# Left operands at fixed products, rows' functions one product later, and a scan that loads behind attention's stores

## The chip, the cores and the metric

The kernel runs on one core of a Trainium2 chip. The metric is the device time of one execution in microseconds (us); less is better. TensorE (PE) multiplies matrices into PSUM; VectorE (DVE), ScalarE (ACT) and GpSimd (POOL) work on rows; SyncE (SP) issues most of the DMA transfers, and POOL a few.

## The reference

One inference step of a hybrid layer, over a prompt of 1024 tokens and a running stream of 64 tokens with a cache, 1088 tokens in all. The width is 1024.

```python
xn = _rmsnorm(x, p['norm_mix_w'])
proj = xn @ p['w_in']
z, xbc, dt_raw, q, k, v, gate_ssm, gate_att = jnp.split(proj, ...)
xbc_c, conv_new = _causal_dwconv(conv_past, xbc, ...)          # then silu, split into xs, bm, cm
y_ssm, ssm_new = _ssd_scan(xs, dt, a_neg, bm, cm, ssm_past, chunk_len)
y_ssm = _rmsnorm((y_ssm + ssm_d * xs) * jax.nn.silu(z), ssm_norm_w)   # by groups
q = _partial_rope(_rmsnorm(q, q_norm_w), q_pos); k = _partial_rope(_rmsnorm(k, k_norm_w), q_pos)
o = _rmsnorm(_diff_attention(q, k_all, v_all, q_pos, k_pos, lam), subln_w)
mix = sigmoid(gate_ssm) * (y_ssm @ w_branch_ssm) + sigmoid(gate_att) * (o @ w_branch_attn)
x = x + mix @ p['w_out']
h = _rmsnorm(x, p['norm_ffn_w']) @ p['w_up']
ha, hb = jnp.split(h, 2, axis=-1)                              # 2816 each
hc, ffn_new = _causal_dwconv(ffn_past, ha, ...)
x = x + (jax.nn.silu(hc) * hb) @ p['w_down']
```

Outputs are x of both parts, the new keys and values, the states of the scan and the last rows of both convolutions, all in float32.

## The kernel before, in words

Everything lies transposed: channels on the 128 partitions, the 1088 tokens along the row, in column halves. To keep float32 precision, an operand is split into a rounded high half and the low rest, and each product is three matmuls (high by high, high by low, low by high). A split is a cast on ACT (the high half) and a subtraction on DVE (the low half); `split` in the code.

The stages, by their time in the profile: values (up to 114 us); the pair stage (114 to 482), which makes z, q and k; attention (to 1083), beside which gates and convolutions run as filler; the scan beside filler (to 1502); branches, output projection and norm (to 1722); the way up of the feed-forward part (to 2189); the way down (to 2436); a tail of stores.

**Pairs.** The pair stage (`in_pair`), the way up (`pair`) and the way down (`down_pair`) multiply 2 × 2 blocks by a Strassen-like scheme with seven products in place of eight. A pair is two blocks of 128 output channels; each of its seven products p runs in two column halves s, so a pair has 14 half products of 12 matmuls. ACT and DVE empty the PSUM tiles into rows u1, u2 and `pre` (L622 to L634 in the pair stage, L1748 to L1770 on the way down), and PE piles a later product on a tile or reuses its bank afterwards. When a row of a pair in the pair stage is whole, `done` takes ACT's Square or Silu, DVE's running sum of squares for q and k, and a store to a scratch in HBM.

**Left operands.** The weights' blocks are loaded as w_f; three sums over them are made (ws1, ws2 and one in place), a fourth later, and seven operands are split: four into rows wh of the tag fa, the others into w_hi and w_lo. In the pair stage and on the way up `left_parts` is a generator that makes one operand after each second half product of the pair before. In the pair stage its DVE part is put off: `split_left` issues the cast at once and keeps the subtraction in `low`, and `low_left` issues it at the next operand (`lagging`). The sums are on POOL from the third pair on (L505, L506, L530, L534). On the way down `down_left` and its `lefts_at` do the same at fixed half products: load at 4, operands 0 to 3 at 8, 10, 11 and 13 of the pair before, operands 4, 5 and 6 at 0, 1 and 3 of the own.

**Rows.** `row(tag, ...)` gives a row from one of two pools: `rows_l` for the tag fa, `rows_r`, on the right side of the memory, for the others (fs for ws1 and ws2, fu for u1 and u2, fp for pre). The right side held the values' staging rows before.

**Jobs.** Between half products `take_turn` lets one or more jobs go on by a step (norm and rope of q and k, their splits); a job yields the number of turns until its next step.

**Scan.** `fetch` loads a span of inputs (tile in, three transfers), `fetch_z` the gate z, `ask` the decay rows (tile bc). `scan` begins with two spans, three asks and two gates (L1170 to L1183). The filler beside attention's end stores gate tiles g_sc (L884) and attention's output o_sc (L1103). The DMA queue of SP takes issues in program order as a scheduler lays them out, so what stands in front and waits holds the rest.

**Way down.** h is stored to the scratch h_sc during the way up. `differences_of` loads two rows of it into tiles ht (tag fb, four buffers), makes four differences on DVE (L1607 to L1610) and stores them to t_sc. The down products take right operands from h_sc (p 0, 2, 6) and t_sc (p 1, 3, 4, 5). There are three groups g of four pairs i, over 8, 8 and 6 blocks of channels; parts for a group are loaded during the last pair of the group before, as m and n tiles and, for the first part of a group, as ph (tag fb too), then split (`landed`). The couples of blocks are counted 0 to 10 in the list, and named by the index of their first block, the last three 16, 17 and 18, all of the third group.

Of the kernel before, what the change touches and what calls it, by code (L numbers as in the profile page):

```python
# [62 lines left out]
IN_ROWS = dict(fs=2, fu=2, fp=3, fc=3, fx=4, ss=2)  # L63
# [27 lines left out]
def hybrid_layer(ctx: ExitStack, tc: tile.TileContext, xT, xt, prm, cst, rope, wvd, win, wbs, wba, wout, wup, wdn,  # L91
# [386 lines left out]

    low, lagging = [], [True]

    def split_left(hi, lo, src):
        S.copy(hi, src)  # L482
        if lagging[0] and "read" in seen:
            low.append((hi, lo, src))
        else:
            V.tensor_tensor(out=lo, in0=src, in1=hi, op=ALU.subtract)  # L486

    def low_left():
        if low:
            with tc.issue_after(seen["read"].ins):  # L490
                for hi, lo, src in low:
                    V.tensor_tensor(out=lo, in0=src, in1=hi, op=ALU.subtract)
            low.clear()

    def left_parts(blocks, early=None, by=G, order=(0, 1, 2, 3)):
# [12 lines left out]
        def own(src):  # L508
            t = row("fa", "wh", R32)
            hi, lo = t[:, :n], t[:, 4 * P : 4 * P + n]  # L510
            split_left(hi, lo, src)
            return hi, lo

        def shared():
            t = [wp.tile([P, wide], R32, name=x, tag=x, bufs=2) for x in ("w_hi", "w_lo")]
            for i, src in enumerate((s1, q22)):
                hi, lo = (x[:, 512 * i : 512 * i + n] for x in t)
                split_left(hi, lo, src)
                yield 4 + i, (hi, lo)
# [16 lines left out]
        split_left(hi, lo, s2)  # L536
        yield 6, (hi, lo)

    def more_left(f):
        low_left()  # L540
        x = next(coming, None)
        if x is not None:
            left.setdefault(f, {})[x[0]] = x[1]

# [21 lines left out]
    def split_part(n, *behind):  # L566
        with ExitStack() as pins:
            for x in behind:
                pins.enter_context(tc.issue_after(x.ins))
            for s in range(2):  # L570
                hi, lo = parts[n, s]
                split(hi, lo, lo.bitcast(F32))

    def in_pair(n):
# [43 lines left out]
        for _ in range(14):  # L618
# [8 lines left out]
            else:  # L627
# [7 lines left out]
                if s == 1:  # L635
                    done(r, c)
# [63 lines left out]
    def job(fetch, scale, hi_of, hi_rows, lo_rows, keep=None):  # L700
# [4 lines left out]
        if scale is not None:  # L705
# [4 lines left out]
            yield 1  # L710
# [4 lines left out]
        yield 2 if keep is None else 3  # L715
# [120 lines left out]
    for p, s in rest:  # L836
        pairs[0].send((p, s))
        if s == 1:
            more_left(1)
            if p in LATER:  # L840
# [4 lines left out]
    for n in range(1, len(INPUT)):  # L845
        coming = in_parts(n + 1) if n + 1 < len(INPUT) else iter(())
# [9 lines left out]
        while n + 1 < len(INPUT) and len(left[n + 1]) < 7:  # L856
            more_left(n + 1)
        low_left()
        del left[n]
        if n == Q_DONE:  # L860
            beside = chain(beside, finishing("q"), finishing("k"))
    while take_turn(0):
        for _ in range(2):
            take_turn(1)
    lagging[0] = False
# [78 lines left out]
    with (tc.tile_pool(name="ak", bufs=1) as ak, tc.tile_pool(name="at", bufs=1) as at,  # L944
# [131 lines left out]
        def head_out(h, o_t, ssq, s0):  # L1076
# [15 lines left out]
            for b0 in range(0, 9, 4):  # L1092
# [9 lines left out]
                for u, t in enumerate((hi, lo)):  # L1102
                    load(out=o_sc[D * u + P * h : D * u + P * (h + 1), b0 * P : b0 * P + w], in_=t.bitcast(F32))  # L1103
# [60 lines left out]
    with (tc.tile_pool(name="sin", bufs=1) as sin, tc.tile_pool(name="sp", bufs=1) as sp,  # L1164
# [343 lines left out]

    ffn_o = tri[:, : 4 * FT].rearrange("p (f c) -> p f c", c=4)
# [144 lines left out]
    made = {}  # L1654

    def down_left(i, what):

        g, m = divmod(i, 4)
        n = P * (DOWN[g] // 2)
        if what == "load":  # L1660
            q = []
            for r in (m, m + 4):
                o = 1024 * first[g] + 2 * n * r
                w = wp.tile([P, wide], F32, name="w_f", tag="w_f", bufs=2)
                load(out=w[:, : 2 * n], in_=wdn[:, o : o + 2 * n])
                q += [w[:, :n], w[:, n : 2 * n]]
            q11, q12, q21, q22 = q
            s1, s2 = (row("fs", x)[:, :n] for x in ("ws1", "ws2"))
            G.tensor_tensor(out=s1, in0=q21, in1=q22, op=ALU.add)
            G.tensor_tensor(out=s2, in0=s1, in1=q11, op=ALU.subtract)  # L1670
            G.tensor_tensor(out=q21, in0=q11, in1=q21, op=ALU.subtract)
            made[i] = [q11, s2, q12, q21, s1, q22, q12]
            left[FT + i] = {}
            return
        src = made[i][what]
        if what < 4:
            t = row("fa", "wh", R32)
            hi, lo = t[:, :n], t[:, 4 * P : 4 * P + n]
        elif what == 6:
            hi, lo = (wp.tile([P, wide], R32, name=x, tag=x, bufs=2)[:, :n] for x in ("w_hi", "w_lo"))  # L1680
        else:
            if len(made[i]) == 7:
                made[i].append([wp.tile([P, wide], R32, name=x, tag=x, bufs=2) for x in ("w_hi", "w_lo")])
            hi, lo = (x[:, 512 * (what - 4) : 512 * (what - 4) + n] for x in made[i][7])
        if what == 3:
            G.tensor_tensor(out=made[i][6], in0=made[i][6], in1=made[i][1], op=ALU.subtract)
        with after("copy", "read"):
            split(hi, lo, src)
        left[FT + i][what] = hi, lo

    def by_token(i):
        return i % 4 in (0, 3)

    def lefts_at(i, at):

        todo = []
        if i >= 0:
# [233 lines left out]
```

## Time and profile before

| | us |
|---|---|
| median of 3 runs | 2461.15 |
| lowest and highest run | 2460.17, 2467.8 |
| the profiled execution's own time | 2447.27 |
| span of the profiled execution | 2445.5 |
| PE busy in the span | 2394.9 (98%) |
| DVE busy | 1744.6 (71%) |
| ACT busy | 1224.1 (50%) |
| POOL busy | 689.0 (28%) |

The profile shows one execution. Its rows of instructions give a start, a duration, the engine, the line and the tiles; where an engine stood idle before an instruction, the time of that and what ended it stand in brackets. A row of waits gives the instruction that waited, the one that ended it, the total us, the number and the longest. A row of transfers gives the count, the size of each and the median us from issue to landing.

### The profile page before, as it was taken

To read this page: it belongs to the slowest core of one execution; us is meant where nothing else is said; L and a number is where in the kernel's file an instruction comes from. 1 tells how busy PE (TensorE), PEld (TensorE's weight loads), DVE (VectorE), ACT (ScalarE), POOL (GpSimd) and SP (SyncE) were. 2 spreads that over 40 slices of the span, in tenths; PEclk is the share of its full clock that TensorE was granted. 3 is DMA by queue.
4 is the path that set the end of the run, shared out by engine and by line. 5 is a ranking of instruction groups with operands and counts; after the bars stand their busy time and mean duration, and the time that the engine had idled before them with its cause. 6 is when DMAs were issued, how large, how long until landed. Compare 5 with 4: busy or idle time off the path is not lost.

```text
span 2445.5 us, 49342 instructions
## 1 busy us (share of the span) xinstructions
PE 2394.9 (98%) x18744; PEld 2319.6 (95%) x18744; DVE 1744.6 (71%) x3118; ACT 1224.1 (50%) x2707; POOL 689.0 (28%) x753
## 2 busy tenths in 40 slices
PE   8999999999999999999999999999999999999998
PEld 8999989999999999998899999999999999999998
DVE  4586867668687786865787665756977777777765
ACT  7354464356565665647665554434543343352442
POOL 0023333201011010104443331013255555534444
PEclk9999999999999999999999999999999999999999
DMA  7855758665445344345897954764123423467876
GB/s 245 283 177 184 241 184 317 219 192 154 152 151 161 123 148 134 114 154 176 270 332 257 339 176 149 218 205 150 58 90 145 154 80 142 150 212 214 220 177 105
DMA packets 283088, 449.79 MB, mean 184 GB/s; under 512 B 35609, under 2 KB 189346, under 8 KB 282850
## 3 DMA queue, kind: packets, MB, share of 16 engines
q1 hardware_dynamic: 271810, 420.30, 51.8%
q0 software_dynamic: 11040, 26.34, 5.4%
q8 instruction: 147, 2.41, 0.4%
q14 instruction: 91, 0.75, 0.1%
HBM read 294.03 MB, written 152.50 MB: 183 GB/s over the span
## 4 chain that ended last, share of the span: by engine, by line
PE 66%; DMA 7%; DVE 7%; issue 3%; POOL 2%; ACT 1%; SPq 0%; POOLq 0%; DVEq 0%; ACTq 0%
PE mx L1528 9%; PE mm L162 9%; PE mm L164 9%; PE mm L163 9%; PE mm L1528 4%; PE mx L1748 4%; PE po L1071 3%; PE mx L164 2%; PE mx L162 2%; PE mx L163 2%; PE mm L1748 2%; PE mx L587 2%; PE sc L1023 2%; PE sc L1022 2%; PE pt L1051 1%
## 5 line engine op out<-in xcount | busy, mean ns | idle before, releaser
L162 PE MATMUL mm<-b,w_hi 128*128 128x272 f32 x1792 | 529.0, 295 | 0.8 <-DVE b_g L230 0.7
L164 PE MATMUL mm<-b,w_lo 128*128 128x272 f32 x1792 | 522.7, 292 | 1.8 <-DVE w_lo L156 1.8
L163 PE MATMUL mm<-b,w_hi 128*128 128x272 f32 x1792 | 520.8, 291 | 0.0
L162 PEld LDWEIGHTS mm<-b,w_hi 128*128 128x128 f32 x1792 | 337.6, 188 | 7.3 <-issue 3.8
L163 PEld LDWEIGHTS mm<-b,w_hi 128*128 128x128 f32 x1792 | 337.8, 189 | 3.3 <-issue 2.6
L164 PEld LDWEIGHTS mm<-b,w_lo 128*128 128x128 f32 x1792 | 337.1, 188 | 3.7 <-DVE w_lo L156 2.4
L912 DVE SCALAR_TENSOR_TENSOR cc<-pre,par,cc 128x272 f32<-128x272 f32 (+1 forms) x288 | 140.1, 490 | 16.4 <-ACT cc L910 13.6
L1528 PE MATMUL mx<-m,w_hi 128*128 128x272 f32 x760 | 146.1, 289 | 1.3 <-ACT m L413 1.3
L1528 PE MATMUL mx<-n,wh 128*128 128x272 f32 x1080 | 144.3, 288 | 1.9 <-DVE u L1555 1.0
L1528 PEld LDWEIGHTS mx<-n,wh 128*128 128x128 f32 x1080 | 138.5, 188 | 2.5 <-DVE u L1555 1.2
L900 POOL COPY pre<-pre 128x3 f32<-128x3 f32 x72 | 22.4, 312 | 418.3 <-DVE cc L914 186.2
L1036 ACT ACTIVATE p_t<-sc,mx 128x512 f32<-128x512 f32 (+6 forms) x144 | 106.1, 739 | 63.4 <-DVE mx L1027 30.9
L156 DVE TENSOR_TENSOR w_lo<-w_f,w_hi 128x1024 fp32r<-128x1024 f32 (+1 forms) x82 | 103.7, 1266 | 46.2 <-ACT w_hi L155 43.5
L155 ACT CAST w_hi<-w_f 128x1024 fp32r<-128x1024 f32 (+1 forms) x82 | 85.9, 1048 | 70.2 <-PE mm L163 43.0
L1528 PEld LDWEIGHTS mx<-m,w_hi 128*128 128x128 f32 x760 | 119.3, 188 | 1.5 <-ACT m L413 1.5
L1545 POOL TENSOR_TENSOR hb<-hb,cc 128x544 f32<-128x544 f32 (+2 forms) x63 | 81.8, 1312 | 101.8 <-DVE hb L1566 50.6
L482 ACT CAST w_hi<-ws 128x512 fp32r<-128x512 f32 x76 | 46.9, 617 | 126.5 <-PE mx L1528 75.0
L1528 PE MATMUL mx<-m,w_lo 128*128 128x272 f32 x380 | 109.7, 289 | 0.0
L1208 ACT ACTIVATE bc<-bc,nacum 128x128 f32<-128x128 f32 (+1 forms) x288 | 87.2, 384 | 16.1 <-POOL bc L1206 15.7
L505 POOL TENSOR_TENSOR ws<-w_f 128x512 f32<-128x512 f32 x34 | 48.5, 1425 | 154.1 <-DMA w_f<-in_win_dram 64.7
L486 DVE TENSOR_TENSOR wh<-w_f,wh 128x512 fp32r<-128x512 f32 x65 | 66.7, 1028 | 26.9 <-ACT wh L482 26.9
L1430 POOL TENSOR_TENSOR s<-s,sq 128x272 f32<-128x272 f32 x24 | 30.5, 1271 | 192.9 <-DMA out_dram<-x 131.2
(467 smaller groups left out, 7093.2 us busy)
## 6 DMA issues: line engine op xcount, KB each, us to landing
w_f<-in_win_dram SPq DMA_DIRECT2D x78, 512.0 KB, 4.2
w_f<-in_wup_dram SPq DMA_DIRECT2D x45, 512.0 KB, 3.4
bc<-a_sc SPq DMA_DIRECT2D x32, 512.0 KB, 5.9
h_sc<-hb SPq DMA_DIRECT2D x44, 272.0 KB, 2.1
ht<-h_sc SPq DMA_DIRECT2D x22, 544.0 KB, 4.8
t_sc<-ht SPq DMA_DIRECT2D x22, 544.0 KB, 2.7
out_dram<-yq POOLq DMA_DIRECT2D x44, 272.0 KB, 5.2
x_sc<-cc SPq DMA_DIRECT2D x72, 136.0 KB, 2.4
```

The lines of the kernel that those rows point to most:

```text
L155: S.copy(hi, w)
L156: V.tensor_tensor(out=lo, in0=w, in1=hi, op=ALU.subtract)
L162: PE.matmul(ps, a_hi, b_hi, start=i == 0, stop=False)
L163: PE.matmul(ps, a_hi, b_lo, start=False, stop=False)
L164: PE.matmul(ps, a_lo, b_hi, start=False, stop=i == n - 1)
L912: V.scalar_tensor_tensor(cc[:, :m], pre[:, i : i + m], cw(i), cc[:, :m], ALU.mult, ALU.add)
L1036: act(p_t[:n, :nk], sc[c][:n, :nk], AF.Exp, bias=mx[:n, c : c + 1], accum_out=dst)
L1071: PE.matmul(po[:n, :P], a_t[b // 4][:kw, b % 4 * P : b % 4 * P + n], rhs, start=b == 0, stop=b == nb - 1)
L1208: act(bc[:L, e, :L], bc[:L, e, :L], AF.Exp, bias=nacum[:L, ch, 8 * g + e : 8 * g + e + 1])
L1528: PE.matmul(ps, w[x][:, c], b[y][:, k], start=start and k == i == 0, stop=k == 3 and i == 2, skip_group_check=not start)
L1545: (V if f + 1 == FT else G).tensor_tensor(out=hb[h][:, o : o + n], in0=hb[h][:, o : o + n], in1=cc[:, d : d + n], op=ALU.mult)
L1748: PE.matmul(ps, w[y][:, c], b[z][:, k], start=start and k == j == 0, stop=k == n - 1 and j == 2, skip_group_check=not start)
```

## The change

- The tags fs and fu come from the left pool `rows_l`.
- `split_left`, `low_left` and `lagging` go. `down_left` and its `lefts_at` become `make_left` and `lefts_at` for all pairs, with the fixed half products of the way down (`short` for the first pair with its own, shorter order). The three first sums follow the load at once; the fourth writes w_f in place of a ws row. The splits are pinned behind the latest evictions ("copy", "read"). The first pairs still use `left_parts`.
- `done` of a row goes into `ripe` and is called one half product later.
- A job yields 2 where it yielded 1 after the scaling, and 2 where k's yielded 3.
- The scan begins with one span and one ask; the second span, asks 1 and 2 and both gates are issued behind the last store of o_sc.
- The differences of the last three couples: 16 was made in the last pair of the way up, 17 and 18 after i = 1 and 2 of the way down; now they are made after i = 2, 3 and 4 in the program's text, and a scheduler places them where their tiles allow.

```diff
-IN_ROWS = dict(fs=2, fu=2, fp=3, fc=3, fx=4, ss=2)
+IN_ROWS = dict(fa=4, fs=2, fu=2, fp=3, fc=3, fx=4, ss=2)
...
-        if tag == "fa":
-            return rows_l.tile([P, KT * P], dt, name=name, tag=tag, bufs=4)
-        w = {"ss": T, "fs": 4 * P}.get(tag, HT)
+        if tag in ("fa", "fs", "fu"):
+            w = {"fa": KT * P, "fs": 4 * P, "fu": HT}[tag]
+            return rows_l.tile([P, w], dt, name=name, tag=tag, bufs=IN_ROWS[tag])
+        w = {"ss": T}.get(tag, HT)
...
+    def make_left(x, what, blocks):
+        if what == "load":
+            q = []
+            for src in blocks:
+                w = wp.tile([P, wide], F32, name="w_f", tag="w_f", bufs=2)
+                n = src.shape[1] // 2
+                load(out=w[:, : 2 * n], in_=src)
+                q += [w[:, :n], w[:, n : 2 * n]]
+            q11, q12, q21, q22 = q
+            s1, s2 = (row("fs", y)[:, :n] for y in ("ws1", "ws2"))
+            G.tensor_tensor(out=s1, in0=q21, in1=q22, op=ALU.add)
+            G.tensor_tensor(out=s2, in0=s1, in1=q11, op=ALU.subtract)
+            G.tensor_tensor(out=q21, in0=q11, in1=q21, op=ALU.subtract)
+            made[x] = [q11, s2, q12, q21, s1, q22, q12]
...
+        if what == 3:
+            G.tensor_tensor(out=made[x][6], in0=made[x][6], in1=made[x][1], op=ALU.subtract)
+        with after("copy", "read"):
+            split(hi, lo, src)
+        left[x][what] = hi, lo
+
+    def lefts_at(x, at, blocks, token_major=lambda x: False, short=False):
+        todo = []
+        if x in made:
+            todo += {0: [(x, 6)]}.get(at, []) if token_major(x) else {0: [(x, 4)], 1: [(x, 5)], 3: [(x, 6)]}.get(at, [])
+        y = x + 1
+        if blocks:
+            mine = {1: "load", 8: 0, 9: 1, 11: 2, 12: 3} if token_major(x) else {4: "load", 8: 0, 10: 1, 11: 2, 13: 3}
+            if short:
+                mine = {0: "load", 4: 0, 6: 1, 7: 2, 9: 3}
...
                 if s == 1:
-                    done(r, c)
+                    ripe.append(lambda r=r, c=c: done(r, c))
...
-            yield 1
+            yield 2
...
-        yield 2 if keep is None else 3
+        yield 2
...
+            old, ripe = ripe, []
             u.send((p, s))
-            if s == 1:
-                more_left(n + 1)
+            for x in old:
+                x()
+            lefts_at(n, at, blocks, short=n == 1)
...
-                    load(out=o_sc[D * u + P * h : D * u + P * (h + 1), b0 * P : b0 * P + w], in_=t.bitcast(F32))
+                    seen["out"] = load(out=o_sc[D * u + P * h : D * u + P * (h + 1), b0 * P : b0 * P + w], in_=t.bitcast(F32))
...
-            got, due = [fetch(*x) for x in spans[:2]], None
-            asked = [ask(*x) for x in steps[:3]]
-            gates = [fetch_z(*x) for x in spans[:2]]
+            got, due = [fetch(*spans[0])], None
+            asked = [ask(*steps[0])]
+            with tc.issue_after(seen["out"].ins):
+                asked += [ask(*x) for x in steps[1:3]]
+                got.append(fetch(*spans[1]))
+                gates = [fetch_z(*x) for x in spans[:2]]
...
-                    if i + n + 2 == f:
+                    if i + n + 2 == f and f + 1 < FT:
                         differences_of(i, n)
...
-        if i in (1, 2):
-            differences_of(*couples[len(couples) - 3 + i])
+        if i in (2, 3, 4):
+            differences_of(*couples[len(couples) - 5 + i])
```

More of the change, by code (lines that the diff above doesn't have):

```diff
@@ L543, in more_left @@
             left.setdefault(f, {})[x[0]] = x[1]
+    made = {}
+    def make_left(x, what, blocks):
[12 more added lines that the diff above has]
+            made[x] = [q11, s2, q12, q21, s1, q22, q12]
+            left[x] = {}
+            return
+        src = made[x][what]
+        n = src.shape[1]
+        if what < 4:
+            t = row("fa", "wh", R32)
+            hi, lo = t[:, :n], t[:, 4 * P : 4 * P + n]
+        elif what == 6:
+            hi, lo = (wp.tile([P, wide], R32, name=y, tag=y, bufs=2)[:, :n] for y in ("w_hi", "w_lo"))
+        else:
+            if len(made[x]) == 7:
+                made[x].append([wp.tile([P, wide], R32, name=y, tag=y, bufs=2) for y in ("w_hi", "w_lo")])
+            hi, lo = (t[:, 512 * (what - 4) : 512 * (what - 4) + n] for t in made[x][7])
+        if what == 3:
+            G.tensor_tensor(out=made[x][6], in0=made[x][6], in1=made[x][1], op=ALU.subtract)
+        with after("copy", "read"):
+            split(hi, lo, src)
+        left[x][what] = hi, lo
@@ new lines, in lefts_at @@
+    def lefts_at(x, at, blocks, token_major=lambda x: False, short=False):
[7 more added lines that the diff above has]
+                mine = {0: "load", 4: 0, 6: 1, 7: 2, 9: 3}
+            if at in mine:
+                todo.append((y, mine[at]))
+            if token_major(y):
+                todo += {13: [(y, 5), (y, 4)]}.get(at, []) if token_major(x) else {12: [(y, 5)], 13: [(y, 4)]}.get(at, [])
+        for y, what in todo:
+            make_left(y, what, blocks)
@@ L1652, in right_parts, with down_blocks @@
             yield
-    made = {}
-    def down_left(i, what):
+    def down_blocks(i):
         g, m = divmod(i, 4)
[L1659 to L1689, printed above, removed]
@@ L1712, in hybrid_layer, with token_major @@
+        return [wdn[:, o : o + n] for o in (1024 * first[g] + n * r for r in (m, m + 4))]
+    def token_major(x):
+        return x + 1 == FT or x >= FT and (x - FT) % 4 in (0, 3)
     add_to = nc.gpsimd.dma_start
```

62 lines of the change are left out of this document (14 added, 48 removed).

## The prediction

> **What bounds the kernel now.** I read the summary first, then the span by stage, then the waits of PE in those stages that the diff touches, then the timeline around the longest of these waits, and the moves of the way down. The summary:
>
> ```profile
> span 2445.5 us, 49342 instructions
> PE 2394.9 (98%) x18744; PEld 2319.6 (95%) x18744; DVE 1744.6 (71%) x3118; ACT 1224.1 (50%) x2707; POOL 689.0 (28%) x753
> ```
>
> PE is busy 2394.9 of 2445.5 us. The change keeps every matmul, so it can win only part of the 50.6 us in which PE stands still, and lose by adding to them. Where they lie, by stage (after the times: the stretch, then busy us of PE, PEld, DVE, ACT, POOL, the clock, DMA share, GB/s):
>
> ```profile
> 114.00:482.00 368.00, 353.44 (x2728) 346.90 (x2726) 278.21 (x466) 178.96 (x324) 108.65 (x104) 0.99 0.65 221
> 1083.00:1203.00 120.00, 113.31 (x893) 102.23 (x893) 76.06 (x94) 72.81 (x183) 44.85 (x29) 0.97 0.65 217
> 1722.00:2189.00 467.00, 462.18 (x3653) 459.60 (x3653) 353.52 (x539) 188.81 (x338) 231.13 (x253) 1.00 0.35 125
> 2189.00:2218.00 29.00, 23.89 (x171) 21.81 (x169) 29.00 (x40) 18.39 (x26) 8.70 (x6) 0.96 0.86 286
> 2218.00:2351.60 133.60, 133.12 (x1040) 132.61 (x1041) 90.39 (x139) 48.33 (x83) 58.15 (x51) 0.98 0.76 188
> 2351.60:2436.00 84.40, 84.38 (x674) 84.15 (x672) 57.27 (x103) 31.66 (x63) 35.88 (x39) 1.00 0.76 167
> ```
>
> Stretch less PE: the pair stage idles 14.6 us, the scan's beginning 6.7, the way up 4.8, the beginning of the way down 5.1, the rest of it 0.5 and 0.0. So some 31 us are within the change's reach, and the last two rows, where PE never waits, can only get worse. The waits behind these sums (pair stage, scan, beginning of the way down):
>
> ```profile
> PE mm L587 <- DVE pre L634: 6.2, 5, 2.8
> PE mx L587 <- DVE pre L634: 5.2, 4, 1.7
> PE mx L587 <- ACT u L622: 2.3, 1, 2.3
> PE mx L162 <- ACT gt L881: 3.9, 1, 3.9
> PE mm L1748 <- ACT yq L1755: 1.8, 1, 1.8
> PE mx L1748 <- DVE m L414: 1.7, 2, 1.1
> ```
>
> All are the same kind: a product's PSUM tile isn't emptied in time, because the engine that empties it is busy or stuck.
>
> **Part 1, rows of the left operands on the left side.** At 123 us:
>
> ```profile
> 123.36 1.25 ACT L622 COPY u<-mx 128x272 f32<-128x272 f32 x4 [7.04 <-DMA out_dram<-vo]
> 123.79 0.69 DVE L505 TENSOR_TENSOR ws<-w_f 128x512 f32<-128x512 f32 x1 [7.18 <-ACT u L622]
> 123.80 0.52 PE L587 MATMUL mx<-b,w_hi 128*128 128x272 f32 x2 [2.35 <-ACT u L622]
> ```
>
> ACT's first copy of a product waits 7.04 us for the store of the values, whose bytes lie where the row u is put; DVE's first sum for the left operand stands 7.18 us behind that; PE stops 2.35 us. With ws and u in the left pool, neither row overlaps the stored tile any longer. PE's 2.35 goes, and with it the backlog of 7 us on DVE, which I put at one later stall of about 1.2 us: −3.5 (between −2.3 and −4). What is late next is pair 1's first u1, which still lies on the right, but it is asked for only after the first six halves of products, at about 124, when the store has landed.
>
> **Part 2, left operands at fixed products, and part 3, rows' functions one product later.** The longest stall of the steady pair stage ends at 342.51:
>
> ```profile
> 335.44 1.78 POOL L530 TENSOR_TENSOR w_f<-w_f 128x512 f32<-128x512 f32 x1
> 339.46 1.40 POOL L534 TENSOR_TENSOR ws<-w_f,ws 128x512 f32<-128x512 f32 x1 [2.25 <-DVE wh L492]
> 339.66 1.50 DVE L787 TENSOR_TENSOR x<-x,rt 128x272 f32<-128x272 f32 x1
> 341.08 0.43 DVE L626 TENSOR_TENSOR u<-mm,u 128x272 f32<-128x272 f32 x1
> 341.43 0.68 DVE L492 TENSOR_TENSOR wh<-w_f,wh 128x512 fp32r<-128x512 f32 x1
> 342.03 0.43 DVE L634 TENSOR_TENSOR pre<-mm,u 128x272 f32<-128x272 f32 x1
> 342.51 0.82 PE L587 MATMUL mm<-b,w_hi 128*128 128x272 f32 x2 [2.82 <-DVE pre L634]
> ```
>
> PE needs the tile that the pre of 342.03 empties. Ahead of it DVE runs a rows' function, 1.50 us long beside the POOL sum (the row below it of the same width takes 0.43), and a left operand's low half, 0.68. A pair has 14 half products, counted 0 to 13. In the changed kernel's instruction order the low halves stand at half products 8 to 13 of the pair before and 0, 1, 3 of the own, each behind the evictions of its product, and the rows' Square, Silu and sums stand behind the next product's evictions. No instruction is added: counts per engine are the same. So 0.68, and often 1.5 more, leave the front of the late eviction. The two rows of waits on pre hold 6.2 + 5.2 = 11.4 us, some 1.2 of it counted above. Of the 10 that are left I take half and a little: −5.5 (between −10 and, with the new placing of POOL's sums, +8, see the third rival). The jobs' yields become 2 where one was 1 and one 3: no work, nothing for PE.
>
> In the way up the same code moves the same instructions; its 4.8 us of idle are spread over its pairs in waits of about 1 us: 0 (−1.5 to +2).
>
> **Part 4, the scan's later loads behind attention's last stores.**
>
> ```profile
> 1082.04 0.86 SPq L1170 DMA_DIRECT2D in<-x_sc  x2
> ...
> 1089.56 2.94 SPq L1183 DMA_DIRECT2D bc<-a_sc  x1
> 1092.60 0.72 SPq L884 DMA_DIRECT2D g_sc<-gt  x1
> 1103.70 0.39 ACT L881 COPY gt<-mx 128x272 f32<-128x272 f32 x1 [11.69 <-DMA g_sc<-gt]
> ```
>
> From 1082.04 on SP issues the scan's first loads, and the gate tile's store only behind the last of them, at 1092.60; ACT stands 11.69 us until a store has landed and frees its tile, and PE 3.9 for ACT. In the changed order three loads of in and one of bc come first, then the stores, then the rest. The store then goes out before the bulk of the loads, 5 us or more earlier, and the 3.9 goes, nearly: −3.5. The other end: asks 1 and 2, span 1 and the two gates now queue behind the last o_sc store on SP, and the scan's second step could wait for them; PE has filler products until then, and if that cover fails it costs up to 2. So −6 to +2.
>
> **Part 5, differences of the last three couples.** Before, couple 16 is made in the last pair up, 17 and 18 in the next pairs, in the row 2189 to 2218, where DVE is busy all 29.00 us. A couple costs DVE four instructions and the queue four moves:
>
> ```profile
> 2190.95 0.72 DVE L1608 TENSOR_TENSOR ht<-ht 128x544 f32<-128x544 f32 x1
> ht<-h_sc SPq DMA_DIRECT2D x6, 544.0 KB, 6.1
> t_sc<-ht SPq DMA_DIRECT2D x6, 544.0 KB, 4.7
> m<-t_sc SPq DMA_DIRECT2D x4, 408.0 KB, 6.6
> m<-h_sc SPq DMA_DIRECT2D x3, 408.0 KB, 10.0
> w_f<-in_wdn_dram SPq DMA_DIRECT2D x8, 384.0 KB, 6.6
> ```
>
> 4 × 0.72 = 2.9 us per couple leave a full DVE; I give PE 4 of its 5.1 us back (−5 to −1).
>
> The price comes later. In the changed order couple 16 runs in the first pair down, but 17 and 18 only in the eighth (i = 7): their four ht tiles share a tag of four buffers with the ph parts of the second group, and these are free only when their products are done:
>
> ```profile
> 2351.59 1.66 PE L1748 MATMUL mm<-m,wh 128*128 128x272 f32 x12
> 2353.08 1.67 PE L1748 MATMUL mx<-ph,wh 128*128 128x272 f32 x12
> 2356.08 1.67 PE L1748 MATMUL mm<-n,wh 128*128 128x272 f32 x12
> ```
>
> Pair 7 starts at T = 2351.59, a half product takes 2353.08 − 2351.59 = 1.49 us, so pair 8 starts 14 × 1.5 = 21.1 later. ph comes free at T + 3.0 and T + 4.5. Loads of ht at T + 4.9 land 6.1 later, at T + 11; the last of eight sums stands behind an eviction of T + 13.5 and ends at about T + 17; the store of t_sc, 4.7, gives T + 22; the third group's load of it, 6.6, gives T + 28.5; its split, about 1, T + 29.5. All eight t_sc parts of that group now wait on SP behind these stores, and two w_f behind them. PE gets through 18 matmuls of h parts in pair 8 and wants the first t_sc part at T + 21.1 + 2.3 = T + 23.4. So it is 6 us late; with stores on an emptier queue a little less, and the seven parts behind come at the pace of the queue, 1 to 4 us more. I take +7.5, between 5.5 (every landing at its best) and 15. In 2351.60 to 2436 before, all of this was hidden, PE idling 0.0 us.
>
> **Sum.** −3.5 − 5.5 + 0 − 3.5 − 4 + 7.5 = −9. The profiled execution took 2447.27 us, of which 2445.5 are the span; the sum makes it 2438. The median of the runs is 2461.15, 14 above it, an offset which I leave as it is: 2461.15 − 9 = 2452.
>
> **Rivals.**
>
> *The late differences cost more than all gains, and it is slower.* Place: i = 7 to 8. If ht, t_sc and the parts land like the m<-h_sc row above, 10.0 each instead of 6.1, 4.7 and 6.6, the chain ends at T + 29.5 + 12.6 = T + 42, 19 late, and DVE, which waits in order on ht, holds back evictions of pair 7 for 2 us more: +21 for +7.5. With −16.5 of gains full it is 4.5 slower, with two thirds of them 10: 2466 to 2471, I say 2469. It decides for slower by over 0.3% when the first t_sc part is ready after about T + 42. For: that stage's rows have landings up to 10.0, eight parts and weights queue together. Against: its DMA share is 0.76, not full, and 6.6 is the row of just these parts. Chance 0.22.
>
> *The late chain is nearly hidden.* The best landings of such moves, here and over the whole span:
>
> ```profile
> ph<-h_sc SPq DMA_DIRECT2D x1, 544.0 KB, 4.0
> t_sc<-ht SPq DMA_DIRECT2D x22, 544.0 KB, 2.7
> ```
>
> If ht and the part land in 4.0, the store in 2.7, and the sums run as soon as ht is there, the chain ends at T + 4.9 + 4.0 + 5 + 2.7 + 4.0 + 1 = T + 21.6, before PE asks. Then +1 stands for +7.5: −15.5, 2446. Against it: the rows of 6.1, 4.7 and 6.6 are of the way down itself and longer. Chance 0.17. The Trainium skill, "DMA: Bandwidth & Descriptors", section "Anatomy of one DMA — SWDGE (gpsimd) path", fits a transfer as about 2.0 us and the bytes over 436 GB/s. By that, as an estimate, 544 KB take 3.3 us and 408 KB 3.0, the chain ends within 1 us of PE's need, and the sum is nearer −15 than −9; the rows of 6.1, 4.7 and 6.6 don't agree with it.
>
> *The steady pair stage loses.* The first three POOL sums now follow the load at once, three in a row of 1.4 to 1.8 us at half products 4 to 8, and DVE works beside them: the row at 339.66 took 1.50 beside POOL's sum. If each DVE instruction there is stretched so, 4.5 us of backlog fall on evictions that have three half products, 4.5 us, until PE needs them; each further low half then stops PE 0.3 us, in 14 pairs +4 instead of −5.5: net +0.5, 2461.5. Chance 0.10. The Trainium skill, "SBUF — State Buffer", section "SBUF: two separate sides", speaks against the change here: a vector operation with two SBUF inputs and a GpSimd operation that reads SBUF take a shared port in turn, and the second waits for the whole first one. The trace agrees in the 1.50 against 0.43.
>
> *It doesn't do what it says.* ACT's first copy still waits (another tile of the right side lies under it, at pair 1) and SP's stores still come late. Then 7 us of gain are missing: −2, 2459. Chance 0.06.
>
> **How the numbers follow.** The forecast, 2452, has 0.45, its own range by the terms' likelier ends 2447 to 2458. A difference under 0.3%, 7.4 us, is about what a measurement of this kernel can tell from none. Faster by more: two thirds of the forecast's 0.45, and the hidden chain's 0.17, 0.47. Slower by more: the first rival's, with a little from the third's tail, 0.23. The rest, 0.30, within. The range goes down through the hidden chain with part 2 at its best, 2442, and up to the first rival's middle, 2468.
>
> **What would show it.** Right: no wait on ACT u L622 near 123; waits on pre in the pair stage at half of 11.4; the wait on gt near 1103 under 0.5; 2189 to 2218 with less than 2 us of PE idle; and a new gap of 5 to 10 us about 21 to 24 us after pair 7's start, ended by the split of a t_sc part. Wrong: that gap above 15 or absent, new stalls at half products 4 to 8 of each pair, or a wait of the scan's second step.

## The result, and the profile after

| | before | after |
|---|---|---|
| median of the runs | 2463.72 us (4 runs) | 2479.22 us (4 runs) |
| lowest and highest | 2460.17, 2467.8 | 2473.57, 2479.98 |
| profiled execution, its span | 2447.27, 2445.5 | 2473.57, 2471.5 |

The ratio is 1.0057, with a 95% interval of 1.0034 to 1.0081: 14 us slower. The forecast was 9 us faster. The profiled execution of before is a quick one, 16 us under its median, that of after is 6 under; so the two spans, 26 us apart, overstate the difference by some 10 us, and single stages are compared below over several profiles.

The summary of the changed kernel:

```profile
span 2471.5 us, 49252 instructions
PE 2400.5 (97%) x18744; PEld 2325.8 (94%) x18744; DVE 1744.3 (71%) x3118; ACT 1224.2 (50%) x2707; POOL 693.0 (28%) x753
```

The instructions of every engine are the same in number, so PE has lost its time in waits and in its clock. The span by stage, cut at the first and last matmul of each (pair stage, scan, way up; the way down counts from the last matmul of the way up), first of before, then of after; the columns are those of the prediction:

```profile
115.24:482.90 367.66, 353.10 (x2724) 346.56 (x2723) 277.64 (x465) 177.72 (x321) 108.65 (x104) 0.99 0.65 221
1080.70:1503.40 422.70, 416.01 (x3344) 379.56 (x3344) 284.68 (x369) 235.85 (x565) 157.79 (x104) 0.99 0.74 248
1724.40:2197.00 472.60, 467.64 (x3699) 465.16 (x3698) 359.12 (x547) 196.08 (x347) 230.69 (x253) 1.00 0.37 129
2197.00:2435.80 238.80, 233.35 (x1821) 230.94 (x1819) 168.46 (x269) 90.37 (x162) 101.41 (x94) 0.99 0.76 187
```

```profile
116.84:493.00 376.16, 356.64 (x2724) 350.68 (x2723) 282.30 (x467) 179.19 (x324) 109.70 (x104) 0.98 0.65 216
1091.06:1509.20 418.14, 412.84 (x3344) 376.75 (x3344) 287.13 (x368) 235.99 (x565) 154.43 (x104) 1.00 0.76 251
1730.20:2200.90 470.70, 466.20 (x3693) 464.26 (x3692) 349.95 (x545) 193.24 (x346) 238.19 (x253) 1.00 0.37 127
2200.90:2461.80 260.90, 239.14 (x1827) 235.35 (x1825) 169.55 (x271) 92.28 (x163) 101.83 (x94) 0.96 0.73 176
```

The pair stage is 8.5 us longer, the scan 4.6 shorter, the way up 1.9 shorter, and the way down 22.1 longer. That last stage decides. The waits of PE there, in the changed kernel:

```profile
PE mm L1743 <- ACT n L413: 6.4, 1, 6.4
PE mx L1743 <- ACT ph L413: 4.6, 1, 4.6
PE mm L1743 <- ACT wh L413: 3.0, 1, 3.0
PE mx L1743 <- DVE yq L1755: 2.6, 1, 2.6
```

Before, nothing of this kind ended a wait over 1.8 us on the way down. The n and ph tiles are right operands of the third group. Here is the chain that the prediction drew, in the timeline of the changed kernel (SP, DVE and ACT at pairs 7 and 8; pair 7 starts at T = 2354.97 there):

```profile
2359.53 2.33 SPq L1650 DMA_DIRECT2D ht<-h_sc  x2
2364.62 0.73 DVE L1652 TENSOR_TENSOR ht<-ht 128x544 f32<-128x544 f32 x1 [5.98 <-DMA ht<-h_sc]
2367.28 4.92 SPq L1657 DMA_DIRECT2D t_sc<-ht  x2
2373.65 0.49 SPq L1678 DMA_DIRECT2D ph<-h_sc  x1
2374.32 0.71 DVE L1655 TENSOR_TENSOR ht<-ht 128x544 f32<-128x544 f32 x1
2375.06 0.32 SPq L1657 DMA_DIRECT2D t_sc<-ht  x1
2381.29 0.37 SPq L1678 DMA_DIRECT2D ph<-t_sc  x1
2382.35 0.87 ACT L413 CAST ph<-ph 128x816 fp32r<-128x816 f32 x1 [2.06 <-DMA ph<-h_sc]
2390.14 0.87 ACT L413 CAST ph<-ph 128x816 fp32r<-128x816 f32 x1 [6.92 <-DMA ph<-t_sc]
```

The loads of ht go out at T + 3 to T + 7 and the last of the eight differences ends at T + 20 (forecast 17). The third t_sc store lands at T + 26 (22) and lets the first t_sc load out, which lands at T + 35 (28.5); the fourth store lands at T + 30. The first t_sc part is split at T + 37 (29.5). PE has run out of parts at 2378.68, T + 23.7. That is near the T + 23.4 of the forecast, but partly by luck: pair 8 began at T + 22.4 in place of 21.1, and PE stopped after 9 of the 18 matmuls on h parts, since the other 9 need ph:

```profile
2377.39 1.29 PE L1743 MATMUL mx<-m,wh 128*128 128x272 f32 x9
2383.27 0.50 PE L1743 MATMUL mx<-ph,wh 128*128 128x272 f32 x1 [4.59 <-ACT ph L413]
2384.32 2.18 PE L1743 MATMUL mx<-ph,wh 128*128 128x272 f32 x8 [0.55 <-DVE ph L414]
2392.89 1.04 PE L1743 MATMUL mm<-n,w_hi 128*128 128x272 f32 x3 [6.39 <-ACT n L413]
```

Two things stand here that the prediction didn't have. The first wait, 4.59, isn't for a t_sc part but for ph<-h_sc. That load carries nothing of the differences, but ph is of the tag fb, whose four buffers the ht tiles hold: SP's record of the load waits on the semaphore of the first t_sc store, issued at 2367.28 and landed at 2373.52, and the load goes out at 2373.65. By itself this wait cost little. Without it, by an estimate from these rows, PE would have stood in one piece from about 2380 to 2392.89, when the first t_sc part that it needs, n, was split. And after the wait eight matmuls take 2.18 us where nine took 1.29 before it: the granted clock, in the windows around the waits,

```profile
2377.00:2378.70 1.70, 1.68 (x14) 1.46 (x12) 1.70 (x3) 0.00 (x0) 1.70 (x3) 1.00 1.07 306
2383.20:2386.50 3.30, 2.68 (x9) 2.05 (x9) 1.01 (x1) 0.02 (x1) 0.00 (x0) 0.53 1.13 250
2392.50:2398.50 6.00, 4.77 (x19) 4.31 (x19) 1.77 (x2) 2.45 (x4) 2.67 (x3) 0.62 1.06 340
```

falls from 1.00 to 0.53 and 0.62. The Trainium skill, "TensorE: Matmul & The Clock Gate", section "Part 1: The HAM clock gate (the "warmup" mystery)", says that TensorE drops to half its clock after some 3.4 us without work and needs as long to come back; the trace agrees, with 0.53 after 4.6 us of idle. So the two waits, 4.6 and 6.4 us, cost more than their sum. Pair 8 took 32.7 us in place of 15.8, pair 9 19.4.

How long the transfers of that stretch took (2350 to 2400, medians), against the 6.1, 4.7 and 6.6 of before:

```profile
ht<-h_sc SPq DMA_DIRECT2D x4, 544.0 KB, 8.2
t_sc<-ht SPq DMA_DIRECT2D x4, 544.0 KB, 7.4
m<-t_sc SPq DMA_DIRECT2D x4, 408.0 KB, 9.2
ph<-t_sc SPq DMA_DIRECT2D x1, 408.0 KB, 8.8
```

### The profile page after: what moved, and what is told of

Same layout as the page of the kernel before. It is cut to its first block, busy times and chain, and to the rows that moved or that the text cites. A ratio compares the mean times of both kernels' runs of the same rounds, so it can differ in the third digit from the quotient of the medians.

```text
span 2471.5 us, 49252 instructions
## 1 busy us (share of the span) xinstructions
PE 2400.5 (97%) x18744; PEld 2325.8 (94%) x18744; DVE 1744.3 (71%) x3118; ACT 1224.2 (50%) x2707; POOL 693.0 (28%) x753
## 4 chain that ended last, share of the span: by engine, by line
PE 75%; DMA 9%; DVE 9%; issue 3%; ACT 2%; POOL 1%; SPq 1%; POOLq 0%; DVEq 0%; ACTq 0%
PE mx L1573 12%; PE mm L162 9%; PE mm L164 9%; PE mm L163 9%; PE mx L626 5%; PE mm L1573 5%; PE po L1112 3%; PE mx L1743 3%; PE mx L162 2%; PE mx L164 2%; PE mx L163 2%; PE mm L626 2%; PE sc L1063 2%; PE sc L1064 2%; PE pt L1092 1%
## 5 line engine op out<-in xcount | busy, mean ns | idle before, releaser
L1077 ACT ACTIVATE p_t<-sc,mx 128x512 f32<-128x512 f32 (+6 forms) x144 | 106.1, 739 | 64.2 <-DVE mx L1068 30.1
L414 DVE TENSOR_TENSOR wh<-w_f,wh 128x512 fp32r<-128x512 f32 (+1 forms) x144 | 130.4, 907 | 10.1 <-ACT wh L413 10.1
L542 POOL TENSOR_TENSOR ws<-w_f 128x512 f32<-128x512 f32 (+1 forms) x46 | 61.1, 1329 | 252.1 <-DMA w_f<-in_win_dram 120.0
L413 ACT CAST wh<-w_f 128x512 fp32r<-128x512 f32 (+1 forms) x144 | 86.9, 611 | 64.0 <-DMA w_f<-in_wdn_dram 25.7
L1584 DVE SCALAR_TENSOR_TENSOR cc<-pre,par,cc 128x544 f32<-128x544 f32 (+1 forms) x88 | 94.7, 1077 | 9.3 <-ACT cc L1582 7.7
L1590 POOL TENSOR_TENSOR hb<-hb,cc 128x544 f32<-128x544 f32 (+2 forms) x63 | 73.6, 1183 | 75.3 <-issue 41.0
```

Of the source, the lines that this page charges most:

```text
L1077: act(p_t[:n, :nk], sc[c][:n, :nk], AF.Exp, bias=mx[:n, c : c + 1], accum_out=dst)
L1584: V.scalar_tensor_tensor(cc[:, :n], pre[h][:, i : i + n], cw(i), cc[:, :n], ALU.mult, ALU.add)
```

## The experiments

Twelve kernels, each in five rounds against the kernel before. Those that start "from after" differ from the changed kernel by their diff alone; "from before" likewise. The table has the ratio to before with its 95% interval, and from each profile the lengths of the pair stage and of the way down.

| run | what it is | ratio | pair stage, us | way down, us |
|---|---|---|---|---|
| – | after | 1.0057 (1.0034 to 1.0081) | 376.2 | 260.9 |
| 1 | after, differences at 0, 1, 2 | 0.9987 (0.9976 to 0.9998) | 377.7 | 240.8 |
| 2 | after without part 5 | 0.9994 (0.9984 to 1.0003) | 379.9 | 241.2 |
| 3 | before + part 5 | 1.0070 (1.0058 to 1.0083) | 370.8 | 259.3 |
| 4 | before + part 4 | 0.9985 (0.9972 to 0.9998) | 369.7 | 243.4 |
| 5 | run 1, old yields | 0.9970 (0.9954 to 0.9985) | 369.5 | 242.6 |
| 6 | run 1 without part 3 | 0.9974 (0.9961 to 0.9987) | 374.9 | 241.2 |
| 7 | run 1, pair stage without part 2 | 0.9976 (0.9964 to 0.9987) | 374.4 | 242.0 |
| 8 | run 1, without 2 and 3 and old yields | 0.9958 (0.9943 to 0.9974) | 371.4 | 240.0 |
| 9 | after, one couple late | 1.0016 (1.0004 to 1.0027) | 376.0 | 246.6 |
| 10 | before + new yields | 1.0023 (1.0011 to 1.0034) | 372.2 | 240.4 |
| 11 | before + part 1 | 0.9987 (0.9975 to 0.9999) | 372.8 | 242.0 |
| 12 | run 8 without part 1 | 0.9958 (0.9944 to 0.9973) | 374.6 | 242.2 |

**Part 5: runs 1, 2, 3 and 9.** Run 1, from after:

```diff
-        if i in (2, 3, 4):
-            differences_of(*couples[len(couples) - 5 + i])
+        if i in (0, 1, 2):
+            differences_of(*couples[len(couples) - 3 + i])
```

> The changed kernel, but the last three couples' differences are asked for after pairs 0, 1 and 2 of the way down in place of 2, 3 and 4, so that all three take their ht tiles before the second group's ph parts do; everything else is as changed. Theory A (the ph parts hold the ht tiles until pair 7, and the third group starves): the waits of PE at pair 8 on splits of t_sc and ph parts, 15 us in the changed kernel's way down, go altogether, its clock there returns from 0.96 to 0.99, the way down takes 238 to 241 us in place of 261, and the time falls by 18 to 22 us, to between 0.3% faster than before and the same. Theory B (the way down is slow because of the left operands' new placing, whose splits and POOL sums the trace shows around the same pairs): the way down stays above 255 us.

Measured: 0.9987, a way down of 240.8 us, and in the profile no wait of PE at all from 2340 to its end. This row is the window from the start of pair 8 on:

```profile
2376.00:2441.00 65.00, 65.00 (x519) 64.77 (x517) 43.78 (x82) 22.59 (x48) 30.51 (x33) 1.00 0.69 128
```

PE is busy 65.00 of 65.00 us at a clock of 1.00. All three couples now take their ht tiles before the last pair of the first group asks for its ph parts, and theory A holds. Against after the ratio is 0.70% lower, some 17 us. A kernel that asks for all three after pair 2 was built but not run; its instructions come out in the same order. So what decides is whether they stand ahead of the ph parts, not the pair's number.

Run 2, from after:

```diff
-                    if i + n + 2 == f and f + 1 < FT:
+                    if i + n + 2 == f:
...
-        if i in (2, 3, 4):
-            differences_of(*couples[len(couples) - 5 + i])
+        if i in (1, 2):
+            differences_of(*couples[len(couples) - 3 + i])
```

> The changed kernel with part 5 alone undone: couple 16's differences in the last pair up, 17 and 18 after pairs 1 and 2 down, as before. Theory A: the way down takes 238 to 242 us, as before; what is left of the change is then the pair stage's (8.5 us longer in the profiled execution), the scan's (4.5 shorter) and the way up's (2 shorter), so the time is within 4 us of the kernel before. If moving the three couples out of the crowded stretch at 2189 to 2218 is worth the 4 us that were forecast, the kernel with pairs 0, 1 and 2 is faster than this one by 3 to 4; if it is worth nothing, they are equal. Theory B: the way down stays above 255.

Measured: 0.9994, way down 241.2. The rest of the change is worth nothing that can be told from no change. Runs 1 and 2 are 0.07% apart with intervals of 0.1%: moving the three couples out of the crowded stretch into the pairs behind it is worth 1 or 2 us, and hardly more than 5. In run 1 the first pair of the way down is 25.8 us long in place of 31.9, but the next four take 93.0 together in place of 87.2 (84.4 is their length without a wait). The differences' moves and sums crowd these pairs instead.

That isn't the gain of part 5 itself, whose couples 17 and 18 leave these pairs too. From the start of the first pair to the start of the sixth, run 3 below takes 114.6 us against 118.0 before, and after takes 116.3 against 119.1 in run 2: some 3 us less. The wait on ACT's wh, 3.0, among the waits above stands in after, but not in runs 3 and 9; what causes it is open.

Run 3, from before, is the reverse:

```diff
-                    if i + n + 2 == f:
+                    if i + n + 2 == f and f + 1 < FT:
...
-        if i in (1, 2):
-            differences_of(*couples[len(couples) - 3 + i])
+        if i in (2, 3, 4):
+            differences_of(*couples[len(couples) - 5 + i])
```

> The kernel before with part 5 alone. Theory A: a gap at the third group's first pair as in the changed kernel, 13 to 17 us of waits and some 5 us of lower clock behind them: 17 to 22 us slower than before (0.7 to 0.9%). Theory B: under 6 us slower.

Measured: 1.0070, and the two largest waits of PE from 2340 on are those of after:

```profile
PE mm L1748 <- ACT n L413: 7.2, 1, 7.2
PE mx L1748 <- ACT ph L413: 3.4, 1, 3.4
```

So part 5 alone costs 17 us (14 to 20), its gain of some 3 already taken off: more than the whole loss.

Run 9, from after, leaves one couple behind the ph parts:

```diff
-        if i in (2, 3, 4):
-            differences_of(*couples[len(couples) - 5 + i])
+        if i in (2, 3):
+            for x in couples[-3:-1] if i == 2 else couples[-1:]:
+                differences_of(*x)
```

> The changed kernel with couples 16 and 17 asked for after pair 2 and only 18 after pair 3: one couple behind the ph parts in place of two. Theory A by its chain: two ht loads may start when pair 7's half product 1 is done, T + 3; they land 5 to 6 us later, four sums of 0.7 us among the evictions end at T + 13 to 15, the store lands at T + 18 to 20, the first t_sc parts at T + 25 to 27 against PE's need at T + 23.4. So PE waits 3 to 9 us in place of 15, the way down takes 243 to 251 us, and the kernel is 0.1 to 0.5% slower than the first experiment's. If the cost were that of moving couples later as such, without the tile, one late couple would cost nothing that can be seen.

Measured: 1.0016, 0.29% or 7 us over run 1; way down 246.6. The waits of PE at pairs 7 to 11:

```profile
PE mx L1743 <- ACT m L413: 4.3, 1, 4.3
PE mm L1743 <- ACT n L413: 1.4, 1, 1.4
```

One couple costs 7 us, two cost 17. With one, two of the four buffers are left for the ph parts, and ph<-h_sc goes out ahead of the stores:

```profile
2360.56 0.37 SPq L1678 DMA_DIRECT2D ph<-h_sc  x1
```

The wait for it is gone; only t_sc parts are late. This is what the chain demands: each couple holds two buffers of the tag, and puts its loads, four sums and two stores in front of the third group's loads on SP. No run gives the tag more than four buffers. So the part that the tile plays is read from where the loads wait (SP's ht loads in after wait for PE's products of pair 7), and from which couples come late.

**Part 4: run 4**, from before, has the change's edit of `scan` and the line that keeps the last o_sc store:

```diff
-            got, due = [fetch(*x) for x in spans[:2]], None
-            asked = [ask(*x) for x in steps[:3]]
-            gates = [fetch_z(*x) for x in spans[:2]]
+            got, due = [fetch(*spans[0])], None
+            asked = [ask(*steps[0])]
+            with tc.issue_after(seen["out"].ins):
+                asked += [ask(*x) for x in steps[1:3]]
+                got.append(fetch(*spans[1]))
+                gates = [fetch_z(*x) for x in spans[:2]]
```

> The kernel before with part 4 alone. If the 4.5 us that the stretch from attention's end to the scan's end is shorter in the changed kernel come from this part: 3 to 5 us faster (0.12 to 0.2%), the wait on gt near 1103 gone, everything else as before. If they come from the executions' spread or from the other order ahead of it: no difference.

Measured: 0.9985, 3.7 us (0.5 to 7) faster. The wait on gt of 3.9 is gone; what is late next is smaller, waits of PE at 1088 to 1205 in this run:

```profile
PE yi L1217 <- DVE y L1225: 3.5, 1, 3.5
PE tr L1196 <- DMA in<-x_sc: 1.9, 2, 1.3
```

**The pair stage: runs 5 to 8.** Each is run 1 with one piece of the pair stage put back. Run 5 the yields, run 6 `done(r, c)` at once, run 7 the generator with `split_left` and `low_left`, run 8 all three:

```diff
# run 5
-            yield 2
+            yield 1
...
-        yield 2
+        yield 2 if keep is None else 3
# run 6
-                    ripe.append(lambda r=r, c=c: done(r, c))
+                    done(r, c)
# run 7
-            lefts_at(n, at, blocks, short=n == 1)
+            if s == 1:
+                more_left(n + 1)
```

> The kernel of the first experiment (differences after pairs 0, 1, 2), with the jobs' yields of the kernel before (1 after the scaling, 3 for k). In the profiles so far the pair stage takes 367.6 to 370.8 us in the kernels with its old code and 376.1 to 379.9 in those with the new. Theory P (the later steps of the jobs free their tile x later, so that the next load of it on POOL, and with it DVE's first instruction on it, come late and hold evictions): the pair stage falls by 4 or more, to under 374, and the waits of DVE on loads of x shrink. Theory Q (the left operands' new places put POOL's sums and low halves on the late evictions): no change, 376 to 380. Theory R (the rows' functions one product later crowd DVE): no change here.

> The kernel of the first experiment with the rows' functions taken at once, as before (part 3 undone). Theory R: the pair stage falls below 374. Theories P and Q: 376 to 380; if the later functions do what they were meant to, it gets longer still.

> The kernel of the first experiment with the pair stage's left operands made as before, by the generator with its put-off low halves (part 2 undone in the pair stage only; the way up keeps the fixed products). Theory Q: the pair stage falls below 374, and the 3 us of PE at 139 on the split of t go too, since the early loads keep their old order. Theories P and R: 376 to 380.

> The kernel of the first experiment with parts 2 and 3 of the pair stage and the yields undone together; of the pair stage's changes only part 1, the pool, is left, and with it the scan's loads, the way up's fixed products and the differences after pairs 0, 1 and 2. The pair stage comes to 367 to 371 us; if part 1 is worth the 2 to 4 us that the wait of ACT at 123 costs, to 364 to 368. In all 8 to 12 us faster than the first experiment's kernel, 0.4 to 0.6% faster than before.

Measured: by time all four are a little faster than run 1, by 0.11 to 0.29%, and can hardly be told apart; run 8's 0.29%, 7 us, is just under its forecast of 8 to 12. By the stage, the yields alone take it back to 369.5; parts 2 and 3 give 3 each, within what one kernel's stage scatters (367.6 to 374.6 in the four profiles whose pair stage is the old code: before, runs 3, 4 and 12; 376.0 to 379.9 in the four that are all new: after, runs 1, 2 and 9). So theory P stands best. A mechanism for q shows in POOL's waits between 284 and 355, where q's jobs run, first after, then run 5; before has no such wait there:

```profile
POOL x L795 <- DMA q_st<-x: 7.5, 3, 3.3
POOL x L811 <- DMA q_st<-x: 7.4, 3, 4.9
```

```profile
POOL rp L812 <- DMA q_st<-rt: 2.5, 1, 2.5
POOL x L811 <- DMA q_st<-x: 2.3, 1, 2.3
```

A job of q ends a turn later than before (2 + 2 turns after the scaling in place of 1 + 2), and so stores its x later; the next job's load of x, on POOL, waits for that store, and DVE, in order, waits for the load with the evictions of the pair behind it. Run 1 shows the worst of it on DVE, where the second slowdown, beside two POOL sums in a row (320.75 to 323.24), adds to the first:

```profile
317.87 0.91 DVE L819 SCALAR_TENSOR_TENSOR x<-x,wq,ss 128x272 f32<-128x272 f32 x2 [4.90 <-DMA x<-q_r]
320.91 2.91 DVE L756 TENSOR_TENSOR x<-x,xh 128x544 fp32r<-128x544 f32 x1
324.38 0.43 DVE L673 TENSOR_TENSOR pre<-mm,u 128x272 f32<-128x272 f32 x1
```

PE stood 5.8 us for that pre.

**Run 10**, from before:

```diff
-            yield 1
+            yield 2
...
-        yield 2 if keep is None else 3
+        yield 2
```

> The kernel before with the new yields alone (2 after the scaling, 2 for k). Theory P: POOL's loads of x wait for the stores of x's low half, as in the changed kernel (14.9 us of such waits between 284 and 355, none before), DVE's first instruction on x comes late, and the pair stage takes 374 to 379 us in place of 368 to 371: 5 to 8 us slower than before, 0.2 to 0.35%. If the yields hurt only together with the new places of the left operands: no change.

Measured: 1.0023, 5.6 us slower: the yields cost this much without any other part. But the place was a miss, and the profile's pair stage, 372.2, lies under the forecast 374 to 379 and inside the scatter of the old code. POOL's waits for q's stores are small here. The longest wait of PE that before doesn't have, 3.0 us near 407, stands in k's jobs, behind a load that POOL issued 9.1 us late:

```profile
402.79 0.54 POOL L756 DMA_DIRECT2D x<-k_r  x1 [9.11 <-DMA k_st<-x]
```

The reason given for q doesn't hold for k, whose job ends as many turns after the scaling as before (2 + 2 in place of 1 + 3), and such waits for k's stores also occur, 12.7 us of them, in run 12 with the old yields. So the cost of the yields is shown by time; the chain by which they cost it is read from traces for q, open for k, and wasn't isolated.

**Part 1: runs 11 and 12.** Run 11 is before with the change's `row`; run 12 is run 8 with `row` as before:

```diff
-        if tag == "fa":
-            return rows_l.tile([P, KT * P], dt, name=name, tag=tag, bufs=4)
-        w = {"ss": T, "fs": 4 * P}.get(tag, HT)
+        if tag in ("fa", "fs", "fu"):
+            w = {"fa": KT * P, "fs": 4 * P, "fu": HT}[tag]
+            return rows_l.tile([P, w], dt, name=name, tag=tag, bufs=IN_ROWS[tag])
+        w = {"ss": T}.get(tag, HT)
```

> The kernel before with part 1 alone, the rows fs and fu on the left. By the prediction: 2.3 to 4 us faster, the pair stage 364 to 367. By the trace of the changed kernel (PE gains 1.8 us up to the 96th matmul of the stage and has lost 3.5 at the 192nd, in a wait of t's split behind DVE's sum on a w_f that lands 24 us after the stage's start either way): the wait at 123 is replaced by one near 139, and the time is the same within 1 us, the pair stage 367 to 371.

> The whole pair stage as before (parts 1, 2, 3 and the yields undone there), with the scan's loads, the way up's fixed products and the differences after pairs 0, 1 and 2. Against the eighth run (the same with part 1): equal within 0.1% if part 1 is worth nothing, 0.1 to 0.15% slower if it is worth the 2 to 4 us of the prediction. Against before: 0.3 to 0.4% faster, by 3 us in the scan, 3 in the way up and 1 to 4 at the beginning of the way down.

Measured: 0.9987 for part 1 alone, barely clear of no change, and 0.9958 both with it (run 8) and without it (run 12). Its worth lies between nothing and 3 us, and stays open within that. The wait that takes its place is plain, DVE and PE of after:

```profile
141.06 0.69 DVE L490 TENSOR_TENSOR ws<-w_f 128x512 f32<-128x512 f32 x1 [3.35 <-DMA w_f<-in_win_dram]
143.01 0.39 PE L626 MATMUL mx<-t,w_hi 128*128 128x272 f32 x1 [3.47 <-DVE t L414]
```

The w_f of pair 1 lands 24 us after the stage's start, where it landed 23 after it before; PE, no longer held at 123, comes to the next wait earlier. At the stage's 96th matmul after is 1.8 us ahead of before, at the 192nd 3.5 behind, at the 576th 1.1 behind. Over all profiles nothing of the lead is left at the 192nd: it starts 26.6 to 29.7 us after the first in the five with the old `row`, and 28.1 to 30.1 in the nine with part 1. Run 11 has the same waits near 139, 2.3 and 1.0.

Runs 8 and 12 are the fastest, 0.42% faster than before (0.26 to 0.57). Run 12 keeps of the change only the scan's loads, the way up's fixed products and the differences off the last pair up. What of its 10 us isn't the scan's 3.7 is the way up's and the differences' together, some 6.5; no run has either alone. The way up, from its first to its last matmul, takes 473.1 to 476.1 us in the nine profiles with fixed products and 477.2 to 482.1 in the five without.

## Why the prediction was wrong

**Two steps failed, by some 12 us each.** The first is the price of part 5, "I take +7.5": it was some +20. By time part 5 costs 17 with its gain of 3 taken off (run 3), and after against run 1 says the same. The mechanism and the place were right: ht behind the ph tiles of the second group, couples in pair 7, PE without parts in pair 8. What was too small is the length of the chain. It was 3 us late after the differences, 4 after the store, 7 when the first t_sc part landed and 8 when it was split. The transfers were priced with rows of the calmer whole stage, 4.7 to 6.6, and took 7.4 to 9.2 in the median; with the differences' eight moves in the same 20 us as the third group's loads, the DMA share is 1.06 to 1.13 in the windows above, where the whole stretch had 0.76. PE's clock, some 4 us, had no term. That the third group's ph tile needs a buffer of ht was not seen either, but that wait lies inside the longer one.

The first rival had the long landings, 10.0 each and T + 42 against T + 37 measured, and its price, +21, is close. Its 2469, set against the median of then, is 8 over before, and 14 came, because it left two thirds of the gains or more standing. In the rival where the chain is nearly hidden, the fit of the Trainium skill, "DMA: Bandwidth & Descriptors", section "Anatomy of one DMA — SWDGE (gpsimd) path", gave 3.0 to 3.3 us a transfer as an estimate. The trace is 4 to 6 us a step over it; the section states the fit for transfers issued from GpSimd, and these went out on SP.

**The second is the pair stage's term**, parts 2 and 3 at −5.5 with the yields at "no work, nothing for PE": together they cost 7 (run 8 against run 1). The yields alone cost +4 to +6 (runs 5 and 10). A yield issues nothing, but it sets when a tile comes free, as the traces show for q. Parts 2 and 3 were no gain: without either, run 1 is some 3 us faster, with intervals that overlap (runs 6 and 7), and the waits on pre came to 9.9 us in after, not to half of 11.4. Ahead of the two longest of these, 3.6 and 2.9, no low half stands any more, as forecast; what stands there are the jobs' instructions. The third rival priced POOL's sums in a row; they were in a row before too (starts at 331.87, 334.19 and 335.44 us), so that this wasn't a change at all, though where a sum meets a late DVE instruction it still stretches it.

**Part 5's gain**, −4, was about right: −3 in the traces.

**Part 1**, −3.5, was 0 to −3: the wait it removes stood in front of another one that ends at the same time after the stage's start. The prediction looked for the next late thing at pair 1's first u1; it was the split of t, behind DVE's sum on a w_f that landed late.

**Part 4**, −3.5, was right: −3.7, and the wait on gt is gone. **The way up**, 0, was better than that, some 4 us faster by the profiles.

The prediction called all the waits that it listed one kind, a PSUM tile not emptied in time. One row, on DVE m L414, 1.7 us, is of another kind: it waits for the split of a right operand.

The terms as measured, +20, +7, −3, −1, −4 and −4, give +15, against the 14 of the runs, with a few us of play in most of them.

## What to carry to other kernels

A step that is moved later takes its buffers later: look in the built order which tile it waits for and who took that tile in between, since here a couple asked for after pair 3 in place of pair 2 ran in pair 7. When a chain ends near its deadline, price it with landings of the stretch into which it moves, filled with its own traffic, and count every load that stands behind its stores on the queue or needs one of its buffers. An edit that issues no work still has a price if it sets when a tile comes free. Removing the first wait of a stage pays only what the next wait, at its own fixed time, leaves over.

## What was not expected of the hardware

After 4.6 us of idle PE's clock was 0.53, and it was back at 1.00 only some 4 us after the second wait. Two windows of after:

```profile
2378.00:2398.00 20.00, 7.97 (x34) 6.82 (x32) 7.36 (x11) 6.79 (x10) 3.92 (x6) 0.66 1.09 331
2398.00:2410.00 12.00, 11.35 (x90) 11.20 (x90) 10.82 (x17) 7.15 (x12) 2.49 (x2) 1.00 0.11 18
```

34 matmuls took 7.97 us of PE in the first, 0.23 us each, and 90 took 11.35 in the second, 0.13 each: some 3.7 us were lost to the clock.

A DVE instruction that takes 0.71 us elsewhere took 2.91 beside two POOL sums in a row (run 1), and one of the same width took 3.29 at the same place in after. Each ended some 0.6 us after the second sum, as if it had waited for both. This agrees with the rule of the Trainium skill that the prediction cites ("SBUF — State Buffer", section "SBUF: two separate sides"), and suggests that two POOL instructions in a row can pass one of DVE.
